# Latents' squares in buffers of their own, four of them summed by TensorE, small inputs and second modulations issued later, in a block of a diffusion backbone on one core

## The chip, the core and the metric

The kernel runs on one core of one Trainium2 chip. A core has five engines with a queue of instructions each, which run beside one another and meet at semaphores: TensorE (PE in the profile; its weight loads are listed apart as PEld) multiplies matrices and writes to PSUM, VectorE (DVE) and ScalarE (ACT) work on vectors, GpSimd (POOL) helps, and SyncE (SP) issues most of the DMAs. The metric is the device time of one execution in microseconds (us); lower is better. Everything is float32.

## The reference

The block has one layer. It takes 512 latent tokens x and 256 context tokens ctx of width 2048, and a condition c with its counterpart c_ctx. What is changed here is the beginning of the layer: RMSNorm of both streams, modulated by adaLN, and the first products of the combined input projection.

```python
mod = (c_act @ w_mod + b_mod)[:, None, :]
mod_c = (cc_act @ w_mod + b_mod)[None, None, :]
sh1, sc1, gt1, sh2, sc2, gt2 = jnp.split(mod, 6, axis=-1)
h = rmsnorm(x, g_norm1) * (1 + sc1) + sh1
hc = rmsnorm(ctx, g_norm1) * (1 + csc1) + csh1
lat_in, lat_gates = project_heads(h, w_in, gla_w_lr, gla_b_lr, mlstm_b_gate)
ctx_in, ctx_gates = project_heads(hc, w_in, gla_w_lr, gla_b_lr, mlstm_b_gate)
```

`rmsnorm` divides each token by the root of the mean of its 2048 squares. `project_heads` is one product with `w_in`, split among four heads of gated linear attention (GLA) and four of mLSTM. Scans over the tokens, an output projection, a SwiGLU MLP with a 3x3 convolution, and a last RMSNorm follow.

## The kernel before

Activations lie with their channels on the partitions: the latents are 16 tiles `xl[k]` of 128 channels x 512 tokens (256 KB each), the context is 8 tiles `xcp[j]` of two channel groups x 256 tokens. An operand of a product is split in two parts, a cast to the matrix format (`hi`) and the rest (`lo`), and each product is three matmuls: hi·hi, hi·lo, lo·hi (`mm3`). ACT makes the cast, DVE the rest, in `split` (L105 and L106).

All matmuls have one line, L111, and are told apart by tiles: `ss_l` and `ss_c` are the sums of squares of latents and context, `ps_m` the modulation products, `a` the projections. The projections' PSUM tiles come from two pools: six banks of `psA`, which hold the sums of head 0 for the whole first stage, and two banks of `psB`, taken in turn by everything else.

The order of the beginning is this.

- SP issues `cv` (the conditions), then two small inputs: the last columns of the constants (`cst`, L515, which hold the column of ones and the selectors) and `cols` (L516, norm weights and biases of the modulation). Then come the 16 latent tiles (L521), the 8 transfers of 512 KB of the first modulation weights (`mod_load`, L277), the first projection weights of head 1 and head 0 (`raw_h`, L195), the context (L419), the second modulation weights, and so on. The weights of each modulation are eight quarter tiles: four for the scale (region 1) and four for the shift (region 0); one such pair serves two channel groups.
- `stream_rstd` (L533) makes the reciprocal root: ACT squares a tile (L537), DVE adds it to a running total (L100), and at the end TensorE multiplies the total by a matrix of ones, which sums over the partitions and spreads the sum (`ss_l`). `mean_rsqrt` follows on ACT and DVE (L174 to L179). The squares take turns in two buffers, tag `sq`; the total has its own, tag `sqs`.
- `mod_rows` multiplies the modulation weights by the conditions (16 matmuls, each with 32 stationary columns and 256 moving ones, four side by side in the array; the page counts two instructions for each), ACT copies the result (L290), `mod_cols` turns it into columns by four small matmuls, and DVE finishes the scale `scol` (L302) or the shift `shcol` (L305).
- `modulate` applies the norm, the scale and the shift to two channel groups of one or both streams (L97, L557, L563) and splits the result into `hTh`, `hTl` (latents) and `hch`, `hcl` (context).
- `project_first` (L408) orders the products. Head 1's first products go through `psB` and are evicted to SBUF sums at once (`early_pair`, `early_group`); head 0's go to `psA` (`project_chunk`). Each has six groups: g = 0, 1 (q and k), 2, 3 (v) use the latents, g = 4, 5 the context. One round of 12 groups is one pair of channel groups (`kp`); there are 8 rounds, each with its own weights and its own pair of modulations.

Within `project_first` every matmul is pinned: TensorE runs them in the order in which the program names them. The other engines' queues are ordered by a planner, which simulates the program and takes an instruction when it is ready by its own estimate, the ones marked with high priority first; `tc.issue_after(ins)` keeps an instruction behind another on the same engine. Each queue then runs strictly in that order.

In the first round the program of before has: pair (g = 0, 1) and groups 2, 3 of head 1; group 0 of head 0; second scale product; group 1; its columns; the context's sum of squares; groups 2, 3; second shift product; group 4 of head 1; its columns; group 5 of head 1; group 4 of head 0; third scale product; group 5; its columns; then the second round.

Of the kernel before, what the change touches and what calls it, by code (L numbers as in the profile page):

```python
# [11 lines left out]
F32 = mybir.dt.float32  # L12
# [6 lines left out]
P = 128  # L19
HW = 256  # L20
D = 2048
KT = D // P
KP = KT // 2
T = 512
# [20 lines left out]
C_SA = C_SEG + T  # L45
# [38 lines left out]
def block_kernel(ctx: ExitStack, tc: tile.TileContext, a: dict, out: bass.AP):  # L84
# [323 lines left out]
    def project_first():  # L408

        banks = [acc(f"a0_{g}", BANKS[g]) for g in range(6)]  # L410
        both = accp.tile([P, CJ, T], F32, name="e0_c", tag="sums")
        early_both.append(both)
        sums = [None] * 4 + [both[:, j, 0 : DK + DV] for j in range(CJ)]
        stream_rstd(xl, rl, "l", T)
        for r in (1, 0):
            mod_cols(r, 0, *mod_rows(r, 0, mod_load(r, 0)))
        w1, w0 = (load_split(a["w_heads"][h, 0], f"h{h}_0") for h in (1, 0))
        for j in range(KT // 2):
            nc.sync.dma_start(xcp[j], a["ctxT"][j])  # L419
        raws = {r: mod_load(r, 1) for r in (1, 0)}  # L420
        with tc.high_priority():
            ins = modulate(0, "x")

        for _ in range(8):
            mm(banks[5][:, 0:P], ones, rl[:, 0:P], start=True, stop=True)
        early_pair(w1, sums)
        for g in range(2, 4):
            early_group(0, g, w1, sums)
        project_chunk(0, *w0, banks[0], 0)
        rows = mod_rows(1, 1, raws[1])  # L430
        project_chunk(0, *w0, banks[1], 1)
        mod_cols(1, 1, *rows)
        with tc.high_priority(), tc.issue_after(ins):
            stream_rstd([x.rearrange("p a b -> p (a b)") for x in xcp], rc, "c", TC)
            ins = modulate(0, "c")
        for g in range(2, 4):
            project_chunk(0, *w0, banks[g], g)
        rows = mod_rows(0, 1, raws[0])
        early_group(0, 4, w1, sums)
        mod_cols(0, 1, *rows)  # L440
        early_group(0, 5, w1, sums)
        with tc.issue_after(ins):
            modulate(1, "xc")
        w1 = load_split(a["w_heads"][1, 1], f"h1_1")
        for r in (1, 0):
            raws[r] = mod_load(r, 2)
        nc.sync.dma_start(cst[:, 0:C_SA], a["consts"][:, 0:C_SA])
        project_chunk(0, *w0, banks[4], 4)
        rows = mod_rows(1, 2, raws[1])
        project_chunk(0, *w0, banks[5], 5)  # L450
        mod_cols(1, 2, *rows)
        for kp in range(1, KP):
            for g in range(6):
                if g == 5 and kp + 1 < KP:
                    rows = mod_rows(0, kp + 1, raws[0])
                ins = early_group(kp, g, w1, sums)
                if g == 2:
                    with tc.issue_after(ins):
                        w0 = load_split(a["w_heads"][0, kp], f"h0_{kp}")
                    if kp + 2 < KP:  # L460
                        raws[1] = mod_load(1, kp + 2)
            if kp + 1 < KP:
                mod_cols(0, kp + 1, *rows)
                with tc.issue_after(ins):
                    modulate(kp + 1, "xc")
            for g in range(6):
                if g == 3 and kp + 2 < KP:
                    rows = mod_rows(1, kp + 2, raws[1])
                project_chunk(kp, *w0, banks[g], g)
                if g == 2 and kp + 1 < KP:  # L470
                    w1 = load_split(a["w_heads"][1, kp + 1], f"h1_{kp + 1}")
                    if kp + 2 < KP:
                        raws[0] = mod_load(0, kp + 2)
                if g == 3 and kp + 2 < KP:
                    mod_cols(1, kp + 2, *rows)
        return banks, sums
# [35 lines left out]
    rstd = xp.tile([P, T + TC], F32, name="rstd")  # L512

    nc.sync.dma_start(cv, a["cvec"])
    nc.sync.dma_start(cst[:, C_SA:], a["consts"][:, C_SA:])  # L515
    nc.sync.dma_start(cols, a["cols"])  # L516
    xl = [ytile(k, f"xl{k}") for k in range(KT)]
    xcp = [actp.tile([P, 2, TC], F32, name=f"xc{j}", tag=f"al{KT // 2 + j}") for j in range(KT // 2)]
    xc = [xcp[k // 2][:, k % 2, :] for k in range(KT)]
    for k in range(KT):  # L520
        nc.sync.dma_start(xl[k], a["xT"][k])  # L521
    S.preload_act_table_set("natural_log_exp_and_others")
    S.activation(ce, cv, AF.Exp, scale=-1.0)
    V.tensor_scalar(out=ce, in0=ce, scalar1=1.0, scalar2=None, op0=ALU.add)
# [6 lines left out]

    def stream_rstd(xs, o, name, n):

        tot = xp.tile([P, T], F32, name=f"sq_{name}", tag="sqs")
        for k, x in enumerate(xs):
            sq = tot if k == 0 else tmp.tile([P, T], F32, name=f"sq_{name}{k}", tag="sq")
            S.activation(sq, x, AF.Square)  # L537
            if k:
                add(tot, tot, sq)
        ps = psb(f"ss_{name}", (P, n))  # L540
        for i in range(0, T, n):
            mm(ps, ones, tot[:, i : i + n], start=(i == 0), stop=(i + n == T))
        var = tmp.tile([P, n], F32, name=f"var_{name}", tag="sq")
        scr = tmp.tile([P, n], F32, name=f"scr_{name}", tag="sq")
        mean_rsqrt(ps, D, var, scr, o)
# [968 lines left out]
```

## Time and profile before

| what | value |
|---|---|
| median of 3 runs | 2444.14 us (2443.68 to 2446.61) |
| the profiled execution's own time | 2443.46 us |
| its span, first to last instruction | 2441.7 us |
| PE busy in the span | 2401.8 us, 98% |
| DVE busy in the span | 1794.5 us, 73% |
| ACT busy in the span | 1003.2 us, 41% |

The profiled execution's own time is 1.76 us above its span (what lies around the first and the last instruction) and 0.68 us below the median of the runs. Times within the span count from its start. In a timeline a row has the start, the busy time, the engine, the line, the operation, the tile written and the tiles read, the count of instructions merged in the row, and in brackets how long the engine was idle before it and what ended that. PE's durations are modelled from the start of a matmul to the end of its pipeline, so a row of one PE instruction overlaps the next; the distance between starts is what it costs in a stream. The chain of waits is followed back from the end: each piece is what the next one waited for.

### The profile page before, as it was taken

The page shows a single profiled execution, that of the slowest core. Times are in us where ns is not written, and L with a number is a line of the kernel's source. Part 1 is how long each engine was busy: PE and PEld are TensorE (multiplying, and loading weights), DVE is VectorE, ACT ScalarE, POOL GpSimd, SP SyncE. Part 2 cuts the span into 40 slices and gives each one's busy share as a digit, 9 for nine tenths or more (in the row PEclk, how much of TensorE's full clock was granted, in tenths as well). Part 3 has the DMA queues.
Part 4 walks back from the last instruction along what each step waited for, and adds up shares of the span by engine and source line. Part 5 has one row for each costly group of instructions (what it writes and reads, how often), then busy time and mean ns, then how long its engine had stood idle before and what let it go on. Part 6 is the DMA issues. An engine that isn't in the chain of part 4 may idle for free.

```text
span 2441.7 us, 38643 instructions
## 1 busy us (share of the span) xinstructions
PE 2401.8 (98%) x15410; PEld 2166.8 (89%) x15410; DVE 1794.5 (73%) x2876; ACT 1003.2 (41%) x1494; POOL 176.3 (7%) x221
## 2 busy tenths in 40 slices
PE   6999999999999999999999999999999999999998
PEld 4888999899988888888898989898999999999997
DVE  6566856655456586769987878878787878787886
ACT  4225533222232232246544444444444444444445
POOL 0000000000000000000101010101011111111021
PEclk9999999999999999999999999999999999999999
DMA  9741111233455788833646464545555555545474
GB/s 384 288 173 56 46 53 44 78 121 113 138 185 191 239 316 279 287 129 111 146 131 154 116 148 124 145 127 138 139 130 142 135 139 126 144 125 151 113 190 130
DMA packets 122487, 373.67 MB, mean 153 GB/s; under 512 B 13912, under 2 KB 19010, under 8 KB 122306
## 3 DMA queue, kind: packets, MB, share of 16 engines
q1 hardware_dynamic: 95298, 318.75, 39.7%
q0 software_dynamic: 25920, 51.40, 11.7%
q8 instruction: 121, 1.98, 0.3%
q10 hardware_dynamic: 1088, 1.05, 0.1%
q14 instruction: 60, 0.49, 0.1%
HBM read 320.80 MB, written 50.34 MB: 152 GB/s over the span
## 4 chain that ended last, share of the span: by engine, by line
PE 84%; issue 6%; DVE 5%; DMA 2%; ACT 1%; POOL 0%; SPq 0%; DVEq 0%; POOLq 0%; ACTq 0%
PE a L111 18%; PE uv L111 16%; PE ug L111 15%; PE dn L111 14%; PE ga L111 7%; PE wo L111 7%; PE po L111 2%; PE ps_m L111 2%; DVE cv L1281 1%; DMA raw_uv<-in_w_up 1%; PE sl L111 1%; DVE lo_d L106 1%; PE st L111 1%; PE cst L111 1%; DVE ex L94 0%
## 5 line engine op out<-in xcount | busy, mean ns | idle before, releaser
L111 PE MATMUL dn<-gh,lo_d 128*128 128x512 f32 x672 | 263.0, 391 | 0.9 <-DVE lo_d L106 0.7
L111 PE MATMUL dn<-gh,hi_d 128*128 128x512 f32 x672 | 261.9, 390 | 0.0
L111 PE MATMUL dn<-gl,hi_d 128*128 128x512 f32 x672 | 261.7, 389 | 0.0
L1281 DVE SCALAR_TENSOR_TENSOR cv<-pads,cwt,cv 128x512 f32<-128x512 f32 x344 | 238.9, 745 | 0.6
L1335 POOL DMA_DIRECT2D x2d<-st x160 | 139.9, 929 | 1141.7 <-ACT st L1334 1061.0
L106 DVE TENSOR_TENSOR lo_buv<-sum_uv,hi_buv 128x1024 fp32r<-128x1024 f32 x80 | 97.9, 1224 | 99.8 <-ACT hi_buv L105 99.7
L322 DVE SCALAR_TENSOR_TENSOR raw_m<-raw_m,crow 128x1024 f32<-128x1024 f32 x128 | 154.6, 1229 | 1.2 <-DMA raw_m<-in_w_mod 1.2
L111 PEld LDWEIGHTS dn<-gh,lo_d 128*128 128x128 f32 x672 | 126.1, 188 | 30.8 <-DVE lo_d L106 4.8
L111 PE MATMUL a<-hi_h,hTh 128*128 128x256 f32 x512 | 151.6, 296 | 0.5 <-ACT e L404 0.5
L111 PEld LDWEIGHTS dn<-gl,hi_d 128*128 128x128 f32 x672 | 126.2, 188 | 26.0
L111 PEld LDWEIGHTS dn<-gh,hi_d 128*128 128x128 f32 x672 | 126.2, 188 | 25.4
L111 PE MATMUL a<-lo_h,hTh 128*128 128x256 f32 x512 | 144.8, 283 | 0.0
L111 PE MATMUL a<-hi_h,hTl 128*128 128x256 f32 x512 | 144.7, 283 | 0.0
L105 ACT CAST hi_d<-raw_d 128x1024 fp32r<-128x1024 f32 x86 | 88.6, 1031 | 132.0 <-PE ug L111 70.3
L106 DVE TENSOR_TENSOR lo_d<-raw_d,hi_d 128x1024 fp32r<-128x1024 f32 x86 | 102.8, 1195 | 48.2 <-ACT hi_d L105 47.5
L111 PE MATMUL ug<-bth,hi_bug 128*128 128x256 f32 x480 | 136.9, 285 | 0.0
L111 PE MATMUL uv<-bth,lo_buv 128*128 128x256 f32 x480 | 136.0, 283 | 0.8 <-DVE lo_buv L106 0.8
L111 PE MATMUL uv<-btl,hi_buv 128*128 128x256 f32 x480 | 135.9, 283 | 0.0
L111 PE MATMUL uv<-bqh,lo_auv 128*128 128x256 f32 x480 | 135.9, 283 | 0.0
L111 PE MATMUL ug<-bqh,hi_aug 128*128 128x256 f32 x480 | 135.9, 283 | 0.0
L111 PE MATMUL ug<-bqh,lo_aug 128*128 128x256 f32 x480 | 135.9, 283 | 0.0
L111 PE MATMUL uv<-bth,hi_buv 128*128 128x256 f32 x480 | 135.9, 283 | 0.0
(410 smaller groups left out, 7245.6 us busy)
## 6 DMA issues: line engine op xcount, KB each, us to landing
raw_m<-in_w_mod SPq DMA_DIRECT2D x192, 512.0 KB, 5.1
raw_d<-in_w_down SPq DMA_DIRECT2D x82, 512.0 KB, 3.5
raw_ug<-in_w_up SPq DMA_DIRECT2D x80, 512.0 KB, 3.5
x2d<-st POOLq DMA_DIRECT2D x160, 256.0 KB, 5.4
raw_uv<-in_w_up SPq DMA_DIRECT2D x80, 512.0 KB, 5.8
raw_h<-in_w_heads SPq DMA_DIRECT2D x64, 512.0 KB, 3.5
raw_ga<-in_w_gates SPq DMA_DIRECT2D x32, 512.0 KB, 3.6
raw_wo<-in_w_out SPq DMA_DIRECT2D x32, 512.0 KB, 4.8
```

What stands on the lines that cost most here:

```text
L105: cast[0] = S.copy(hi, x).ins
L106: return V.tensor_tensor(out=lo, in0=x, in1=hi.bitcast(F32), op=ALU.subtract).ins
L111: ins = PE.matmul(*args, **kw)
L322: V.scalar_tensor_tensor(out=x, in0=x, scalar=1.0, in1=crow[0], op0=ALU.mult, op1=ALU.mult, accum_out=mtot[:, at : at + 1])
L1281: V.scalar_tensor_tensor(out=t3, in0=src, scalar=w, in1=t3, op0=ALU.mult, op1=ALU.add)
L1335: nc.gpsimd.dma_start(x2d[k], t, accum_op=ALU.add)
```

## The change

- In `stream_rstd`, the latents' 16 squares get a buffer each. They are buffers of `actp` that later hold the split operands (`ah2` to `ah11` and `al2` to `al7`). The total is kept in the first of them. DVE adds the squares 1 to 11; the last four are not added. TensorE multiplies each of those by the ones itself and accumulates: squares 12, 13, 14, then the total, then square 15, five matmuls of 512 columns for one before. The context's eight squares are summed as before.
- The DMAs of `cst` (last columns) and `cols` are issued behind the 16 latent tiles, ahead of the modulation weights.
- In the first round TensorE's order becomes: pair and groups 2, 3 of head 1; groups 0, 1, 2 of head 0; the context's sum of squares; second scale product; group 3; its columns; group 4 of head 1; second shift product; group 5 of head 1; its columns; groups 4, 5 of head 0. The third scale product goes into the second round, behind its groups 0 and 1; its columns come behind group 2.

```diff
--- before.py
+++ after.py
@@ -426,34 +426,35 @@
         early_pair(w1, sums)
         for g in range(2, 4):
             early_group(0, g, w1, sums)
-        project_chunk(0, *w0, banks[0], 0)
-        rows = mod_rows(1, 1, raws[1])
-        project_chunk(0, *w0, banks[1], 1)
-        mod_cols(1, 1, *rows)
+        for g in range(3):
+            project_chunk(0, *w0, banks[g], g)
         with tc.high_priority(), tc.issue_after(ins):
             stream_rstd([x.rearrange("p a b -> p (a b)") for x in xcp], rc, "c", TC)
             ins = modulate(0, "c")
-        for g in range(2, 4):
-            project_chunk(0, *w0, banks[g], g)
+        rows = mod_rows(1, 1, raws[1])
+        project_chunk(0, *w0, banks[3], 3)
+        mod_cols(1, 1, *rows)
+        early_group(0, 4, w1, sums)
         rows = mod_rows(0, 1, raws[0])
-        early_group(0, 4, w1, sums)
+        early_group(0, 5, w1, sums)
         mod_cols(0, 1, *rows)
-        early_group(0, 5, w1, sums)
         with tc.issue_after(ins):
             modulate(1, "xc")
         w1 = load_split(a["w_heads"][1, 1], f"h1_1")
         for r in (1, 0):
             raws[r] = mod_load(r, 2)
         nc.sync.dma_start(cst[:, 0:C_SA], a["consts"][:, 0:C_SA])
-        project_chunk(0, *w0, banks[4], 4)
-        rows = mod_rows(1, 2, raws[1])
-        project_chunk(0, *w0, banks[5], 5)
-        mod_cols(1, 2, *rows)
+        for g in (4, 5):
+            project_chunk(0, *w0, banks[g], g)
         for kp in range(1, KP):
             for g in range(6):
                 if g == 5 and kp + 1 < KP:
                     rows = mod_rows(0, kp + 1, raws[0])
+                if kp == 1 and g == 2:
+                    rows = mod_rows(1, 2, raws[1])
                 ins = early_group(kp, g, w1, sums)
+                if kp == 1 and g == 2:
+                    mod_cols(1, 2, *rows)
                 if g == 2:
                     with tc.issue_after(ins):
                         w0 = load_split(a["w_heads"][0, kp], f"h0_{kp}")
@@ -512,13 +513,13 @@
     rstd = xp.tile([P, T + TC], F32, name="rstd")
 
     nc.sync.dma_start(cv, a["cvec"])
-    nc.sync.dma_start(cst[:, C_SA:], a["consts"][:, C_SA:])
-    nc.sync.dma_start(cols, a["cols"])
     xl = [ytile(k, f"xl{k}") for k in range(KT)]
     xcp = [actp.tile([P, 2, TC], F32, name=f"xc{j}", tag=f"al{KT // 2 + j}") for j in range(KT // 2)]
     xc = [xcp[k // 2][:, k % 2, :] for k in range(KT)]
     for k in range(KT):
         nc.sync.dma_start(xl[k], a["xT"][k])
+    nc.sync.dma_start(cst[:, C_SA:], a["consts"][:, C_SA:])
+    nc.sync.dma_start(cols, a["cols"])
     S.preload_act_table_set("natural_log_exp_and_others")
     S.activation(ce, cv, AF.Exp, scale=-1.0)
     V.tensor_scalar(out=ce, in0=ce, scalar1=1.0, scalar2=None, op0=ALU.add)
@@ -531,15 +532,26 @@
 
     def stream_rstd(xs, o, name, n):
 
-        tot = xp.tile([P, T], F32, name=f"sq_{name}", tag="sqs")
+        tot, tail = None, []
         for k, x in enumerate(xs):
-            sq = tot if k == 0 else tmp.tile([P, T], F32, name=f"sq_{name}{k}", tag="sq")
+            if len(xs) == KT:
+                tag = f"ah{2 + k}" if k < 10 else f"al{k - 8}"
+                sq = actp.tile([P, T], F32, name=f"sq_{name}{k}", tag=tag)
+            elif k == 0:
+                sq = xp.tile([P, T], F32, name=f"sq_{name}", tag="sqs")
+            else:
+                sq = tmp.tile([P, T], F32, name=f"sq_{name}{k}", tag="sq")
             S.activation(sq, x, AF.Square)
-            if k:
+            if k == 0:
+                tot = sq
+            elif k < 12:
                 add(tot, tot, sq)
+            else:
+                tail.append(sq)
         ps = psb(f"ss_{name}", (P, n))
-        for i in range(0, T, n):
-            mm(ps, ones, tot[:, i : i + n], start=(i == 0), stop=(i + n == T))
+        parts = [x[:, i : i + n] for x in tail[:-1] + [tot] + tail[-1:] for i in range(0, T, n)]
+        for i, part in enumerate(parts):
+            mm(ps, ones, part, start=(i == 0), stop=(i + 1 == len(parts)))
         var = tmp.tile([P, n], F32, name=f"var_{name}", tag="sq")
         scr = tmp.tile([P, n], F32, name=f"scr_{name}", tag="sq")
         mean_rsqrt(ps, D, var, scr, o)
```

## The prediction, made before the changed kernel was run

> **What bounds the kernel now.** I read the page first, then the waits of TensorE at the beginning, the timelines of DVE and ACT there, the landing of transfers, and last the chain of waits up to the second round.
>
> ```profile
> span 2441.7 us, 38643 instructions
> PE 2401.8 (98%) x15410; PEld 2166.8 (89%) x15410; DVE 1794.5 (73%) x2876; ACT 1003.2 (41%) x1494; POOL 176.3 (7%) x221
> ```
>
> TensorE is busy for 98% of the span, so it sets the time, and only what makes it wait counts. The change touches the first 60 us. These are TensorE's waits of the first 140 us (waiter, releaser: total, times, longest):
>
> ```profile
> PE ss_l L111 <- DVE sq_l L100: 19.4, 1, 19.4
> PE ps_m L111 <- ACT rows_m L290: 1.0, 2, 0.5
> PE a L111 <- ACT e L404: 0.5, 1, 0.5
> PE a L111 <- ACT e_c L390: 0.2, 1, 0.2
> ```
>
> Half of the 40 us without PE lie before the first matmul; after that under 2 us. So the question is by how much the stream of products starts earlier, and which waits come up behind it. First the squares, from ACT's and DVE's timelines:
>
> ```profile
> 3.50 0.56 DVE L589 CAST glr<-cst 2x768 fp32r<-2x768 f32 x1 [0.21 <-DMA cst<-in_consts]
> 9.26 2.02 ACT L537 ACTIVATE sq_l<-xl 128x512 f32<-128x512 f32 x3 [0.37 <-DMA xl<-in_xT]
> 17.81 0.63 ACT L537 ACTIVATE sq_l<-xl 128x512 f32<-128x512 f32 x1 [0.17 <-DVE sq_l L100]
> 9.92 9.45 DVE L100 TENSOR_TENSOR sq_l<-sq_l,sq_l 128x512 f32<-128x512 f32 x12 [0.30 <-ACT sq_l L537]
> 19.43 2.07 PE L111 MATMUL ss_l<-sq_l,cst 128*128 128x512 f32 x2 [19.43 <-DVE sq_l L100]
> 21.43 3.64 PE L111 MATMUL ps_m<-raw_m,cact 128*32 128x256 f32 x32
> 26.10 1.93 PE L111 MATMUL ps_m<-raw_m,cact 128*32 128x256 f32 x32
> 30.78 0.99 PE L111 MATMUL a<-hTh,hi_h 128*128 128x512 f32 x3
> 27.08 0.27 DVE L302 TENSOR_SCALAR scol<-ps_m,bp,cols 128x2 f32<-128x2 f32 x1
> ```
>
> DVE makes 12 adds in 9.45 us, 0.79 each. ACT, which first waits for the tiles, waits for DVE to free a buffer by its last square. The sum ends at 21.5; two modulation products follow, and the projections start at 30.78. The first modulation product took 3.64 us, the second, with the same 32 instructions, 1.93: TensorE is slow at first, by a factor of 1.89, and stays so from 19.43 to the last of 3.64 us of matmuls, some 5.4 us, at most 26.10-19.43=6.7. (The profile's granted clock is 1.00 there, so this slowness isn't in it.)
>
> Next the transfers: SP's issues, each followed by its KB and us to landing; then DMA share and GB/s in a table by stretch.
>
> ```profile
> 1.27 0.42 SPq L515 DMA_DIRECT2D cst<-in_consts  x1
> 2.21 9.21 SPq L521 DMA_DIRECT2D xl<-in_xT  x16
> 11.09 0.33 SPq L521 DMA_DIRECT2D xl<-in_xT  x1
> xl<-in_xT SPq DMA_DIRECT2D x1, 256.0 KB, 5.2
> 16.26 0.33 SPq L277 DMA_DIRECT2D raw_m<-in_w_mod  x1
> raw_m<-in_w_mod SPq DMA_DIRECT2D x1, 512.0 KB, 10.1
> cols<-in_cols SPq DMA_DIRECT2D x1, 74.0 KB, 2.0
> cst<-in_consts SPq DMA_DIRECT2D x1, 80.5 KB
> 20.00:30.00 10.00, 9.02 (x83) 4.33 (x82) 5.26 (x12) 3.01 (x5) 0.00 (x0) 1.00 1.03 416
> 30.00:60.00 30.00, 29.30 (x242) 23.67 (x241) 21.71 (x44) 15.86 (x30) 0.00 (x0) 1.00 1.03 415
> ```
>
> The last latent tile lands at 11.09+5.2=16.3, the last of the first eight modulation weights at 16.26+10.1=26.4, and the DMA engines are full throughout. That is the second limit: TensorE can't finish its second modulation product before 26.4 plus a last quarter (1.93/4=0.5).
>
> **The change part by part.**
>
> *Small inputs behind the latents.* The latents are issued 2.21-1.27=0.94 us earlier, so the last one lands at about 15.35. The two small inputs (154.5 KB) take about 0.4 us of the stream at 416 GB/s, so the ones land at 15.6 and the modulation weights at 26.4-0.94+0.4=25.85. Their readers: DVE's L530 and a cast at L589, which the planner may place among the adds (rival 1), and TensorE, whose sums can't start before the ones, at 15.6.
>
> *Squares in their own buffers.* ACT no longer waits for DVE: it follows the landings at 2.02/3=0.67 us a square and ends at 16.0 to 16.3. DVE has 11 adds: the fourth starts at 9.92-0.94=9.0, the eleventh ends at 9.0+8x0.79=15.3, 4.1 us earlier than 19.4. The buffers' later owners are operands of the second round, after 50 us.
>
> *Four squares on TensorE.* The same sum over 512 columns by ss_c, once TensorE is fast, costs 0.97 us (chain of waits, below); times 1.89 that is 1.83 cold, a little under the 2.07 of the lone one. Five run from 15.6. If TensorE stays cold for 5.4 us as before, until 21.0, then 5.4/1.83=2.95 are done, and 2.05x0.97=2.0 more end at 23.0. So the sum ends 1.5 us *later* than at 21.5, though the adds end earlier. The first modulation product is then fast, 1.93 for 3.64, which wins 1.7 back: the second starts 0.2 before 26.10, at 25.9, where its weights (25.85) just don't hold it. DVE's norm, from 21.5 to 27.35 before (its last interleaved row, 27.08+0.27), ends 1.5 later at 28.9, when the shift arrives. So the projections start 0.2 earlier, at 30.6. Ends: 1.1 earlier, if TensorE is fast so soon that the weights bind (their 25.85+0.5 and the product before it make the second end at 26.9, not 28.03); 0.1 later if it stays cold for 6.7 us.
>
> By the Trainium skill, page "TensorE: Matmul & The Clock Gate", Part 1, cold time is about 3.4 us of sustained activity, counted by a free-running window. The trace's 5.4 us is longer. By 3.4 the projections would start 1.1 us earlier instead of 0.2 (rival 2).
>
> *Second modulations moved.* TensorE's work is the same, so only new waits cost. The rows are pieces of the chain of waits (start, us) and DVE's timeline:
>
> ```profile
> 38.81 1.86 PE ps_m L111 x32
> 42.26 0.34 PE ps_m L111 x4
> 42.60 0.97 PE ss_c L111 x4
> 43.57 2.86 PE a L111 x24
> 46.44 1.86 PE ps_m L111 x32
> 49.58 0.50 ACT e_c L390
> 50.12 2.35 PE a L111 x12
> 52.48 1.86 PE ps_m L111 x32
> 54.34 1.24 PE a L111 x6
> 55.92 6.76 PE a L111 x42
> 47.06 0.73 ACT L105 CAST hch<-xc 128x256 fp32r<-128x256 f32 x2 [2.53 <-DVE xc L563]
> 47.50 0.76 DVE L106 TENSOR_TENSOR hcl<-xc,hch 128x256 fp32r<-128x256 f32 x2
> 50.05 0.34 DVE L305 TENSOR_SCALAR shcol<-ps_m,cols 128x2 f32<-128x2 f32 x2
> 52.93 1.23 DVE L106 TENSOR_TENSOR lo_h<-raw_h,hi_h 128x1024 fp32r<-128x1024 f32 x1 [0.37 <-ACT hi_h L105]
> 54.41 0.68 DVE L106 TENSOR_TENSOR hTl<-xl,hTh 128x512 fp32r<-128x512 f32 x1
> ```
>
> Their weights: all DMA slots are refilled as the stream needs them, since the issue runs 10 us ahead of the landing; products that come 2 to 4 us later use up a part of that lead, so I cost the queue on SP at nothing (if that lead were gone, each late transfer would cost its 1.26 us, 512 KB at 416 GB/s).
>
> The context first. Its chain runs from the end of ss_c, 43.57, to the first cast, 47.06+0.4, 3.9 us, and to the last rest, 48.26, 4.7 us. Before, two groups and a product cover it (2.86+1.86=4.7). After, there are a product, a group and the columns, 1.86+1.43+0.34=3.63, so group 4 of head 1 waits 0.25. In exchange the wait of 0.24 for the eviction e_c goes, since a modulation product now stands between groups 4 and 5.
>
> The latents' second pair of channel groups is the larger item. Before, shcol starts at 50.05 and the last hTl ends at 54.41+0.68=55.09, 5.04 us later, of which DVE works 4.67 and stands 0.37 for hi_h; the second round starts at 55.92, behind it. After, group 0 of head 0 ends at 38.8-0.2=38.6; +1.43+1.43+0.97 is 42.4, the end of ss_c. Group 4 starts at 42.4+3.9=46.3 and takes 1.17 (half of 2.35); +1.86 (shift product) +1.17 (group 5) +0.34 gives 50.8 for the columns. The cast hi_h needs the buffer that group 5 frees, which now comes earlier and fills the 0.37, so hTl ends at 50.8+4.67=55.5. Between the columns and the second round TensorE now has two groups, 2.4 us; before it had two more items, 1.86 and 0.34, and group 5. It reaches the round at 53.2 and would end its first group at 53.2+1.43=54.6 (a latents' group is half of 2.86); the last two of six matmuls wait for hTl and end at 55.5+0.48=56.0. That is a new wait of 1.35. Its ends: 0.6, where lo_h (1.23) is queued behind both hTl; 2.2, where the context's parts (four of 0.4) all come first and the 0.37 stays. Behind it come the moved third product and its columns, 2.2, so the point that was reached at 55.92+1.43=57.35 is reached at 58.2.
>
> *Sum.* -0.2 (start) +0.25 (context) -0.24 (e_c) -0.3 (gaps at switches between products, in the chain of before and not in my lengths) +1.35 (latents' operands) = +0.86, as 58.2-57.35. From there on TensorE streams as before. Against the profiled execution's 2443.46 this gives 2444.3; the median of the runs lies 0.68 above that execution, so 2445.0.
>
> **The rivals.** 0.2% is 4.9 us, and about what a measurement of this kernel can tell from no change.
>
> 1. *Small inputs block the adds (slower).* DVE takes its queue in order. If the planner puts L530 and L589 ahead of the adds, DVE stands until cols lands, about 15.8, then needs 0.7 for the two and 11x0.79=8.7: 25.2. Two sums follow, 1.9 fast or 3.7 cold: 27.1 to 28.9, so 5.6 to 7.4 later than 21.5, less 1.7 for a fast modulation product in the first case: +3.9 to +7.4. With the waits further on that is +5 to +8.5, 2449.1 to 2452.6. It decides only with more than five adds behind the two, since TensorE takes up the total at 15.6+3x1.83=21.1, and (21.1-16.5)/0.79=5.8. Against it: L589's row shows that the planner's landing of cst was right to 0.21 us, so it should see that squares are ready long before cols. The Trainium skill, same page and part, states that DVE and ACT are strict FIFO; the trace agrees, L589 held DVE for those 0.21 us.
> 2. *Fast early, operands early (a little faster).* The projections start 1.1 earlier instead of 0.2, and lo_h comes behind both hTl: 0.86-0.9-0.75=-0.8, 2443.3. No change by the bound.
> 3. *The squares bring nothing.* TensorE is cold for 6.7 us (+0.3) and DVE's scol of the second scale (two of 0.27) comes into the middle of the context's chain (+0.5): 0.86+0.8=1.7, 2445.8. Also no change.
> 4. *Another order far behind.* The planner sees a shifted beginning and orders ACT and DVE otherwise in the 2380 us that follow; nothing in the profile prices it, in either sign.
>
> **How the numbers follow.** Forecast 0.55, rival 2 0.15, rival 3 0.12: together 0.82, all within 0.2%. Rival 1: 0.09, slower. Rival 4 beyond the bound: 0.05 faster, 0.04 slower. Range: rival 2's 2443.3 less 2 for an order that differs behind, 2441.2; at the top it reaches rival 1's lower end, 2449.1. The forecast's own range, from the ends of its terms (-0.9 and -0.75, +0.3, +0.5 and +0.85), is 2443.3 to 2446.6.
>
> **What would show it.** Right: ACT's squares without DVE waits, ending near 16.3; ss_l as ten instructions from about 15.6 to 23; the first modulation product near 1.9 us; the projections at 30 to 30.7; a new wait of TensorE for hTl or lo_h at 53 to 55. Wrong: an idle DVE released by cst or cols among the adds; ss_l beyond 25; a DMA share below 1 before 60 us; a second round that starts with no wait.

## The result, and the profile after

The median after is 2448.05 us (20 runs, 2445.87 to 2451.57); before, on the same chips, 2443.40 (20 runs, 2440.58 to 2446.81). The ratio is 1.0016, 95% interval 1.0010 to 1.0022. By the ratio that is 3.9 us slower (2443.4 x 0.0016, from 2.4 to 5.4); the two medians themselves differ by 4.65. Both are inside the 0.2% (4.9 us) that counts as no change, and inside the predicted range, near its upper end. But the interval excludes no difference: the kernel after is slower, by less than the bound. The forecast difference was +0.86, so some 3 us came from something that the sum doesn't hold. First the page of the kernel after (span, then busy time by engine):

```profile
span 2446.6 us, 38631 instructions
PE 2407.6 (98%) x15418; PEld 2170.4 (89%) x15418; DVE 1793.0 (73%) x2872; ACT 1002.9 (41%) x1494; POOL 176.2 (7%) x221
```

These are TensorE's waits in its first 140 us (waiter, releaser: total, times, longest); the two rows that are as before, for `rows_m` and ACT's `e`, are left out:

```profile
PE ss_l L111 <- DMA cst<-in_consts: 15.4, 1, 15.4
PE a L111 <- DVE hTl L106: 1.0, 1, 1.0
...
PE a L111 <- DVE lo_h L106: 0.7, 1, 0.7
...
PE a L111 <- DVE e L392: 0.4, 1, 0.4
PE a L111 <- ACT hi_h L105: 0.2, 1, 0.2
PE a L111 <- DVE hcl L106: 0.2, 1, 0.2
```

TensorE's share is the 98% it was. The first wait is 4 us shorter (15.4 for 19.4) and that of 0.2 for `e_c` is gone, but five new ones stand behind. One of them, for `hTl`, is the one that the prediction priced. Now the beginning in the timelines of ACT, DVE and TensorE (start, length, engine, line, operation, tiles, count, idle time before):

```profile
6.54 9.17 ACT L544 ACTIVATE sq_l<-xl 128x512 f32<-128x512 f32 x14 [1.30 <-DMA xl<-in_xT]
7.21 7.86 DVE L100 TENSOR_TENSOR sq_l<-sq_l,sq_l 128x512 f32<-128x512 f32 x10 [1.24 <-ACT sq_l L544]
15.42 7.39 PE L111 MATMUL ss_l<-sq_l,cst 128*128 128x512 f32 x10 [15.42 <-DMA cst<-in_consts]
22.73 1.93 PE L111 MATMUL ps_m<-raw_m,cact 128*32 128x256 f32 x32
25.70 1.93 PE L111 MATMUL ps_m<-raw_m,cact 128*32 128x256 f32 x32
30.38 0.99 PE L111 MATMUL a<-hTh,hi_h 128*128 128x512 f32 x3
```

ACT runs through its squares without a wait for DVE and ends at 15.7, DVE's adds end at 15.07, the five sums run from 15.42 to 22.8, and the first modulation product is a fast one. The projections start at 30.38, 0.40 earlier than before. All of that is as forecast. The time is lost later, in the second round. These are some starts of TensorE's matmuls there, first of the kernel before:

```profile
55.78 0.48 PE L111 MATMUL a<-hTh,hi_h 128*128 128x512 f32 x1
58.37 0.39 PE L111 MATMUL a<-hTh,lo_h 128*128 128x512 f32 x1
60.02 0.28 PE L111 MATMUL a<-hi_h,hTh 128*128 128x256 f32 x1
65.98 0.48 PE L111 MATMUL a<-hTh,hi_h 128*128 128x512 f32 x1
66.52 0.39 PE L111 MATMUL a<-hTh,lo_h 128*128 128x512 f32 x1
```

and the same five matmuls of the kernel after, with the one that waits between the first and the second:

```profile
53.31 0.39 PE L111 MATMUL a<-hTh,hi_h 128*128 128x512 f32 x1
54.75 0.50 PE L111 MATMUL a<-hTl,hi_h 128*128 128x512 f32 x1 [1.05 <-DVE hTl L106]
57.40 0.39 PE L111 MATMUL a<-hTh,lo_h 128*128 128x512 f32 x1
62.06 0.39 PE L111 MATMUL a<-hi_h,hTh 128*128 128x256 f32 x1 [0.45 <-DVE e L392]
68.49 0.50 PE L111 MATMUL a<-hTh,hi_h 128*128 128x512 f32 x1 [0.23 <-ACT hi_h L105]
69.96 0.50 PE L111 MATMUL a<-hTh,lo_h 128*128 128x512 f32 x1 [0.73 <-DVE lo_h L106]
```

At the first two marks the kernel after still owes the third scale product and its columns, 1.86+0.36=2.22 us, which the kernel before has behind it; from the fourth row on they are done in both. So its position against before is 53.31+2.22-55.78=-0.25 at the start of the round, 57.40+2.22-58.37=+1.25 behind the wait for `hTl`, 62.06-60.02=+2.04 behind the wait for the eviction `e`, 68.49-65.98=+2.51 behind the wait for `hi_h`, and 69.96-66.52=+3.44 behind that for `lo_h`. (Each wait costs more than the idle time in brackets: in a stream, rows of 0.39 start 0.23 apart, so an overlap of 0.16 is lost as well, and the row behind the wait is one of 0.50.) So four waits in 17 us make nearly the whole loss. Why `lo_h` is late is seen in the queues of ACT and DVE. Before:

```profile
58.70 1.05 ACT L105 CAST hi_h<-raw_h 128x1024 fp32r<-128x1024 f32 x1 [3.92 <-DMA raw_h<-in_w_heads]
63.19 1.22 DVE L106 TENSOR_TENSOR lo_h<-raw_h,hi_h 128x1024 fp32r<-128x1024 f32 x1
65.82 0.56 DVE L392 SCALAR_TENSOR_TENSOR e_c<-a,e_c 128x384 f32<-128x384 f32 x1 [1.41 <-PE a L111]
```

After, with the copy of the modulation's rows ahead of the cast:

```profile
51.37 0.35 DVE L305 TENSOR_SCALAR shcol<-ps_m,cols 128x2 f32<-128x2 f32 x2 [2.36 <-PE ps_m L111]
67.12 0.37 ACT L290 COPY rows_m<-ps_m 128x256 f32<-128x256 f32 x1 [6.97 <-PE ps_m L111]
67.39 1.05 ACT L105 CAST hi_h<-raw_h 128x1024 fp32r<-128x1024 f32 x1
67.95 0.56 DVE L392 SCALAR_TENSOR_TENSOR e_c<-a,e_c 128x384 f32<-128x384 f32 x1 [2.55 <-PE a L111]
68.69 1.22 DVE L106 TENSOR_TENSOR lo_h<-raw_h,hi_h 128x1024 fp32r<-128x1024 f32 x1
```

Before, head 0's weights of the second round are cast when they land, at 58.70, and split at 63.19, between the two evictions. After, the planner has put the cast behind the copy of the third shift product's rows. ACT stands 6.97 us for that product with the cast queued behind it, and the rest `lo_h` stands on DVE behind the second eviction, for which DVE is idle for 2.55. No engine is short of time here: it is the order in two queues.

The position can also be read in one row: the start of the last of nine modulation products that lie between 70 and 160 us, the same one in every kernel. Before, then after (matmuls, their shortest/median/longest ns, first and last start):

```profile
L111 PE MATMUL ps_m<-raw_m,cact x288: 378/379/404, 70.3 to 154.0; 128*32 128x256 f32 x144
```

```profile
L111 PE MATMUL ps_m<-raw_m,cact x288: 379/379/403, 73.9 to 157.7; 128*32 128x256 f32 x144
```

After is 3.7 us behind at that mark, and its time 3.9 longer by the ratio (an interval of 2.4 to 5.4): what follows the mark adds nothing that the times could show.

### The profile page after: what moved, and what is told of

Its sections match the earlier page's. It is cut to its first block, busy times and chain, and to the rows that moved or that the text cites. A ratio compares the mean times of both kernels' runs of the same rounds, so it can differ in the third digit from the quotient of the medians.

```text
span 2446.6 us, 38631 instructions
## 1 busy us (share of the span) xinstructions
PE 2407.6 (98%) x15418; PEld 2170.4 (89%) x15418; DVE 1793.0 (73%) x2872; ACT 1002.9 (41%) x1494; POOL 176.2 (7%) x221
## 3 DMA queue, kind: packets, MB, share of 16 engines
q10 hardware_dynamic: 1088, 1.05, 0.1%
## 4 chain that ended last, share of the span: by engine, by line
PE 82%; issue 10%; DVE 4%; DMA 2%; ACT 1%; POOL 1%; SPq 0%; DVEq 0%; POOLq 0%; ACTq 0%
PE a L111 17%; PE dn L111 16%; PE uv L111 16%; PE ug L111 15%; PE ga L111 7%; PE wo L111 3%; PE po L111 2%; PE ps_m L111 1%; PE sl L111 1%; PE st L111 1%; PE cst L111 1%; DMA raw_m<-in_w_mod 1%; DVE cv L1293 0%; DVE ex L94 0%; DMA xl<-in_xT 0%
## 5 line engine op out<-in xcount | busy, mean ns | idle before, releaser
L111 PEld LDWEIGHTS dn<-gl,hi_d 128*128 128x128 f32 x672 | 126.2, 188 | 25.9
```

What stands on the lines that cost most here:

```text
L111: ins = PE.matmul(*args, **kw)
```

## The experiments

My theory was that the order of the second modulations costs some 4 us by three mechanisms (shift columns late for the second round; a PSUM bank; the order of cast, rest and evictions), and that the squares win a few tenths. The rivals were that the squares and small inputs cost something themselves, and that the planner orders the later stages otherwise (the prediction's rival 4). All runs together (start of the projections in the profile; position by the starts of equal matmuls against before at 75 us; span; median; ratio with interval, where there were several rounds):

| kernel | start | position | span | time | ratio |
|---|---|---|---|---|---|
| before | 30.78 | 0 | 2441.7 | 2443.40 | 1 |
| after | 30.38 | +3.6 | 2446.6 | 2448.05 | 1.0016 (1.0010 to 1.0022) |
| sq_only | 30.20 | -0.3 | 2440.2 | 2444.16 | 0.9997 (0.9988 to 1.0006) |
| order_only | 30.09 | +3.3 | 2445.4 | 2446.94 | 1.0008 (0.9999 to 1.0017) |
| third_back | 30.30 | +1.4 | 2442.1 | 2448.10 | 1.0011 (1.0002 to 1.0020) |
| cast_first | 30.10 | +3.8 | 2444.4 | 2450.10 | 1.0020 (1.0011 to 1.0029) |
| lo_first | 29.67 | +1.4 | 2445.8 | 2447.55, one run | |
| before_again | 30.31 | -0.1 | 2445.8 | 2447.51, one run | |
| sq_dve | 29.36 | -0.1 | 2443.6 | 2445.83, one run | |
| sq_warm | 29.63 | -0.7 | 2441.7 | 2443.38, one run | |
| mid_dve | 29.42 | -1.3 | 2441.9 | 2442.47 | 0.9996 (0.9987 to 1.0004) |
| mid_warm | 29.15 | -1.6 | 2442.1 | 2444.33 | 0.9997 (0.9988 to 1.0006) |

Each ratio is to the runs of the kernel before on the same chip, whose medians were 2443.40 (20 runs, beside the kernel after), 2444.03 (33 runs, the four from `sq_only` to `cast_first`), 2443.75 (one run, the four single ones) and 2444.74 (21 runs, the last two). The intervals are about 0.09% either way, 2.2 us (0.06% for the kernel after); single runs differ by more, for a reason that `before_again` shows. So mechanisms are judged by positions and waits, and the medians only by whether they agree.

**sq_only**: the squares and the small inputs as in the kernel after, `project_first` as before.

> The changed kernel with the old order of products in the first two rounds; the squares and the small inputs stay as changed. Theory (the loss comes from the moved modulation products): the projections start 0.4 us earlier than before, at 30.4, the second round starts at about 55.5, its head 0 part at 65.7 (before: 66.12), and from there TensorE stays 0.2 to 0.5 us ahead of the kernel before; time -0.4 us, no change. Rival (the squares and small inputs cost it, by a later sum or a disturbed DMA stream): head 0's part of the second round starts 3 to 4 us after 66.12, as in the changed kernel.

```profile
L111 PE MATMUL ps_m<-raw_m,cact x288: 379/379/403, 70.0 to 153.7; 128*32 128x256 f32 x144
```

The mark comes at 153.7, 0.3 earlier than before, and none of the new waits is there. The squares don't cost, and hardly win.

**order_only**: the reverse, the new order with the old squares and inputs. The edit of this and of `sq_only` is the two halves of the change:

```diff
@@ project_first: as after in order_only, as before in sq_only
-        project_chunk(0, *w0, banks[0], 0)
-        rows = mod_rows(1, 1, raws[1])
-        project_chunk(0, *w0, banks[1], 1)
-        mod_cols(1, 1, *rows)
+        for g in range(3):
+            project_chunk(0, *w0, banks[g], g)
...
@@ stream_rstd and the DMAs of cst and cols: as before in order_only, as after in sq_only
```

> The kernel before with the new order of products alone. Theory: the three new waits all appear (hTl 1.5 us, eviction 0.6, weights' cast 1.5), from 75 us on TensorE is 3.9 to 4.2 us behind the kernel before, time +4 us or a little more. Rival (squares and small inputs): within 0.5 us of the kernel before.

The waits and the mark of `order_only`:

```profile
PE a L111 <- DVE hTl L106: 1.1, 1, 1.1
PE a L111 <- DVE lo_h L106: 1.0, 1, 1.0
...
L111 PE MATMUL ps_m<-raw_m,cact x288: 379/379/403, 73.6 to 157.3; 128*32 128x256 f32 x144
```

The same waits but the small one for `hi_h`, and 3.3 us behind at the mark. The order alone makes the loss: counted from the start of the projections it is 3.3+0.7=4.0 here and 3.6+0.4=4.0 in the kernel after. (The time, with an interval from 0.9999 to 1.0017, would not show it.) At the mark it is smaller than I expected, since this execution started 0.7 earlier than that of before (30.09 against 30.78) with the same instructions up to there: the start varies by itself (`before_again` has 30.31), so the 0.40 that after starts earlier is no proof of a gain either.

**third_back**: from the kernel after, only the third scale product and its columns put back to where before has them.

```diff
-        for g in (4, 5):
-            project_chunk(0, *w0, banks[g], g)
+        project_chunk(0, *w0, banks[4], 4)
+        rows = mod_rows(1, 2, raws[1])
+        project_chunk(0, *w0, banks[5], 5)
+        mod_cols(1, 2, *rows)
```

> The changed kernel with the third scale product and its columns back between and behind groups 4 and 5 of head 0. Theory: the wait for hTl shrinks to 0, the wait for an eviction at 61 and the one for the weights' cast at 68 go (its cast stands ahead of the copy of the third shift product on ACT again), so from 75 us on TensorE is 0 to 0.5 us ahead of the kernel before; time -0.2 us. Rival (the second products' places alone cost it, by the context's chain): still 1 us or more behind.

Its ACT and TensorE around 56 us, and the mark:

```profile
55.92 0.40 ACT L105 CAST hch<-xc 128x256 fp32r<-128x256 f32 x1 [2.26 <-DVE xc L573]
56.23 0.37 ACT L290 COPY rows_m<-ps_m 128x256 f32<-128x256 f32 x1
56.65 0.61 PE L111 MATMUL ps_m<-cst,rows_m 128*128 128x2 f32 x4 [1.18 <-ACT rows_m L290]
...
L111 PE MATMUL ps_m<-raw_m,cact x288: 379/379/403, 71.7 to 155.4; 128*32 128x256 f32 x144
```

This removes the waits for `hTl`, for the eviction and for `lo_h` at a stroke, 2.2 us of the loss, but I had expected it to remove all of it. The copy of the product's rows now stands on ACT behind the last cast of the context, at the end of the same chain from the shift columns (here at 51.30), and TensorE waits 1.18 for the copy. So that chain takes its toll wherever TensorE first meets it. This part of the loss belongs to the second products, which lie later than before, not to the third one. That `third_back` is faster than the kernel after rests on the positions: its median is 4.1 us above that of before, and its interval, 1.0002 to 1.0020, holds a loss of 1.4 us as well as one of 3.9.

**cast_first**: from the kernel after, the copy of the third shift product's rows goes behind the cast `hi_h` of head 0 in ACT's queue.

```diff
-        with tc.high_priority():
+        with tc.high_priority(), behind(queue):
             S.copy(rows, ps)
...
-                    rows = mod_rows(0, kp + 1, raws[0])
+                    rows = mod_rows(0, kp + 1, raws[0], (cast[0],) if kp == 1 else ())
```

> The changed kernel with one order edge on ACT: the copy of the third shift product's rows queues behind the cast hi_h of head 0's second weights. Theory (that cast stood behind the copy though its weights had landed 9 us before): the wait of 1.5 us at 68 goes, the other two stay, and from 75 us on TensorE is 2.0 to 2.3 us behind the kernel before instead of 3.6. Rival (the cast waits for its weights or its buffer): no difference, 3.6.

```profile
59.81 1.05 ACT L105 CAST hi_h<-raw_h 128x1024 fp32r<-128x1024 f32 x1
67.70 0.56 DVE L392 SCALAR_TENSOR_TENSOR e_c<-a,e_c 128x384 f32<-128x384 f32 x1 [2.55 <-PE a L111]
68.91 1.22 DVE L106 TENSOR_TENSOR lo_h<-raw_h,hi_h 128x1024 fp32r<-128x1024 f32 x1
...
L111 PE MATMUL ps_m<-raw_m,cact x288: 379/379/403, 74.1 to 157.9; 128*32 128x256 f32 x144
```

A miss. The cast comes at 59.81, 7.6 us earlier, and TensorE isn't served any sooner: on DVE the rest is still queued behind the second eviction, which starts at 67.70 after 2.55 idle, and now also behind another instruction that the planner put ahead of it (`xl`, L97, 0.68 us from 68.18). The mark is 3.9 behind; counted from the start of the projections this is 0.5 worse than the kernel after. So the cast's place alone is not the cause.

**lo_first**: `cast_first`, and the second of the two evictions behind the rest `lo_h` in DVE's queue.

```diff
-                ins = early_group(kp, g, w1, sums)
+                ins = early_group(kp, g, w1, sums, (parted[0],) if (kp, g) == (1, 5) else ())
```

> The kernel of cast_first with one more order edge, on DVE: the eviction of group 5 of head 1 in the second round queues behind the rest lo_h of head 0's second weights. Theory (DVE stood idle before 67.7 with lo_h behind an eviction that waited for TensorE): lo_h runs near 63, TensorE's wait of 1.6 us for it at 70 goes, and from 75 us on TensorE is 1.5 us less behind than in cast_first: 2.3 us behind the kernel before (start counted alike) instead of 3.8. Rival (lo_h is late for another reason): no difference.

```profile
64.63 1.22 DVE L106 TENSOR_TENSOR lo_h<-raw_h,hi_h 128x1024 fp32r<-128x1024 f32 x1
...
L111 PE MATMUL ps_m<-raw_m,cact x288: 378/379/404, 71.8 to 155.4; 128*32 128x256 f32 x144
```

The rest is made at 64.63 in the 2.55 us in which DVE stood idle, the wait for `lo_h` is gone, and the mark comes 2.5 us earlier than in `cast_first`, of which the start accounts for 0.43. That is some 2 us against `cast_first`; against the kernel after the two edges together win 1.4 (1.4+1.1=2.5 us behind, counted from the start, for 4.0), the step from 2.04 to 3.44 above. It was paid for instructions in the wrong order in two queues with idle time, and the cast had to come early too: in the kernel after it ends only at 68.44.

**before_again**: the kernel before, unchanged, once more with a profile, to see what two executions of one program differ by.

> The kernel before, unchanged, to see how far the same program's beginning moves from one execution to another. If the start of the projections (30.78 in the first profile, 30.09 in the run with the new order alone, whose beginning is the same program) moves by 0.7 us by itself, the gain that the squares bring at the start can't be read to better than that. Expected: projections between 30.0 and 30.8, the same distances between TensorE's products behind them.

The mark, and then two stretches far behind in a table (bounds, length, busy time of PE, PEld, DVE, ACT and POOL with instructions, PEclk, the DMA share and GB/s):

```profile
L111 PE MATMUL ps_m<-raw_m,cact x288: 378/379/404, 70.2 to 154.0; 128*32 128x256 f32 x144
470.00:477.60 7.60, 6.99 (x59) 6.38 (x58) 6.67 (x22) 1.99 (x7) 0.00 (x0) 1.00 0.22 69
477.60:481.10 3.50, 3.50 (x11) 3.13 (x11) 1.69 (x8) 1.48 (x3) 0.00 (x0) 0.52 0.00 0
```

and the second of the two stretches in the first execution of before:

```profile
477.60:481.10 3.50, 3.50 (x18) 3.04 (x18) 2.35 (x8) 1.48 (x3) 0.00 (x0) 1.00 0.00 0
```

From the second round to 477 us the two agree within 0.1 us. There the granted clock falls to 0.52 for 3.5 us in one of them (11 matmuls for 18), which costs 1.6, and the same happens around 1075 us, for 2.3. At the end the spans differ by 4.1, with nothing changed. Every trace but the first of before has such a step at one or both of these places (after has one of 1.4 near 1075), so what a single span shows behind 450 us says nothing about a change of this size, and an order that differs far behind isn't needed to explain the times.

**sq_dve**: `sq_only`, with all sixteen squares added by DVE, one sum on TensorE.

```diff
-            elif k < 12:
+            elif k < 12 or len(xs) == KT:
```

> The kernel of sq_only with all sixteen squares of the latents added by DVE again, in their own buffers; one sum on TensorE. Theory (five sums on a cold TensorE take longer than DVE's four adds): DVE ends its adds at 18.2, the one sum runs from 18.3 to 20.4, 2.1 us earlier than the 22.6 of sq_only, the first modulation product is slow again (3.6), and the projections start 0.4 to 0.8 us earlier than in sq_only, at 29.4 to 29.8. Rival (it is the weights' landing alone that sets the start): no difference, 30.2.

Its second scale product, and the mark:

```profile
39.88 0.64 PE L111 MATMUL ps_m<-raw_m,cact 128*32 128x256 f32 x8 [0.59 <-DMA raw_m<-in_w_mod]
...
L111 PE MATMUL ps_m<-raw_m,cact x288: 379/379/403, 70.2 to 154.0; 128*32 128x256 f32 x144
```

The start is at 29.36 (29.42 in `mid_dve`, which begins alike), 0.8 earlier than in `sq_only` and 0.3 to 1.0 earlier than in the five executions with four squares on a cold TensorE. The adds ended at 18.6, 0.4 later than I expected, because the planner put the cast of a small input (L600, 0.56 us from 17.31) ahead of the last add: rival 1 of the prediction, in small. But nothing of the early start is left at the mark. The second scale product, in its old place, now waits for its weights, and its last quarter starts at 39.88, when the full stream of transfers has delivered it. This is the limit behind the limit: with the old order, most of an earlier start is handed to the next transfer.

**sq_warm**: `sq_only`, with eleven products of latent tiles ahead of the sums, whose results nothing reads.

```diff
+        for k in range(2, 13):
+            mm(banks[5][:, 0:256], xl[k][:, 0:P], xl[k][:, 0:256], start=True, stop=True)
```

> The kernel of sq_only with eleven small products of latent tiles, whose result nobody reads, ahead of the sums, so that TensorE is fast when the sums come. Theory: the five sums take 0.97 each, from 15.4 to 20.3, the first modulation product ends at about 22.2, and the second is bound by the landing of its last weights at 25.7: it ends at 26.2 and the projections start at 28.9, 1.3 earlier than in sq_only. The second scale product then waits for its weights at 39.6 (up to 1.2 us), so that at 75 us no more than 0.5 us of it are left. Rival (TensorE isn't slow for lack of use): sums of 1.8 as before, start 30.2.

```profile
16.03 4.53 PE L111 MATMUL ss_l<-sq_l,cst 128*128 128x512 f32 x10 [1.33 <-DMA cst<-in_consts]
26.25 0.64 PE L111 MATMUL ps_m<-raw_m,cact 128*32 128x256 f32 x8 [0.59 <-DMA raw_m<-in_w_mod]
```

The five sums take 4.53 us for 7.39, as the reading of a cold TensorE foretells. The gain is then cut at the next landing, as I had expected, but the last quarter could start only at 26.25, for weights expected at 25.7, and the start is 29.63 for 28.9. (That the second modulation product is held by its weights is the prediction's other end for the start.) At the mark 0.7 are kept, more than expected, since the second scale product waits less here: its last quarter starts at 39.36, for 39.88 in `sq_dve`.

**mid_dve** and **mid_warm**: these put the two findings together. The beginning is that of `sq_dve` or `sq_warm`; of the second modulations only the scale product moves, by one group, so that its weights have landed, and the shift product with its columns stays where before has it.

```diff
-        project_chunk(0, *w0, banks[0], 0)
-        rows = mod_rows(1, 1, raws[1])
-        project_chunk(0, *w0, banks[1], 1)
-        mod_cols(1, 1, *rows)
+        for g in range(2):
+            project_chunk(0, *w0, banks[g], g)
...
-        for g in range(2, 4):
-            project_chunk(0, *w0, banks[g], g)
+        rows = mod_rows(1, 1, raws[1])
+        project_chunk(0, *w0, banks[2], 2)
+        mod_cols(1, 1, *rows)
+        project_chunk(0, *w0, banks[3], 3)
```

> All sixteen squares added by DVE in buffers of their own, small inputs behind the latents, and of the second modulations only the scale product moved: from between the groups 0 and 1 of head 0 to between 1 and 2, its columns behind 2; everything else as in the kernel before. Theory (with the old order an early start is given back at the second scale product, because its last weights land at 39.2 to 39.9 whatever the start; the shift columns may not come later): projections start at 29.2 to 29.9, no wait of the second scale product for its weights, no wait of over 0.5 for hTl or lo_h, and the lead is kept: 0.8 to 1.4 us ahead of the kernel before at 75 us. Time 0.03 to 0.06% shorter, within the interval. Rival (the lead is lost anyway, at the shift columns and the operands of the second round): a new wait for hTl or lo_h of about 1, and within 0.3 us of the kernel before at 75 us.

> The same order (second scale product one group later than before) with the last four squares on TensorE and eleven unread products of latent tiles ahead of the sums. Theory: projections start at 29.5 to 29.9, no wait of the second scale product for its weights, 0.8 to 1.3 us ahead of the kernel before at 75 us; the time 0.03 to 0.06% shorter, within the interval. Rival: the lead of 0.65 that the old order kept with the same beginning stays as it is, because another wait comes up for hTl or lo_h.

The mark of `mid_dve`, then of `mid_warm` (some records are missing in both; the last start is the same product's):

```profile
L111 PE MATMUL ps_m<-raw_m,cact x276: 379/379/403, 69.6 to 152.7; 128*32 128x256 f32 x138
```

```profile
L111 PE MATMUL ps_m<-raw_m,cact x268: 379/379/403, 69.8 to 152.4; 128*32 128x256 f32 x134
```

No wait for `hTl`, `lo_h` or the weights of the second scale product is left, and the lead is kept: 1.3 and 1.6 us at the mark. So a move of the second modulations can help, by one group of one of them. As a time it is 0.05 to 0.07% and not to be told from none (0.9996, interval 0.9987 to 1.0004, and 0.9997, 0.9988 to 1.0006): faster than the kernel before is not shown. Against the kernel after, the intervals of the ratios don't overlap (up to 1.0006 here, from 1.0010 there), and the positions are 5 us apart.

## Why the prediction was right or wrong

The forecast, no measurable change at +0.86, holds by the bound and not by its sum: the loss is over four times the forecast one, and that it stays below 4.9 us is luck. The bound was also called about what a measurement can tell from no change; this one, of 20 runs, tells 3.9 us from none. Point by point:

- *Small inputs and squares*: right in each step. The ones landed for the sums at 15.42 (predicted 15.6), ACT ended at 15.7 (16.0 to 16.3), DVE's adds at 15.07 (15.3), and neither `cst` nor `cols` held up an add, so rival 1 didn't occur.
- *Four squares on TensorE*: right. The sums ended at 22.8 (23.0), later than before; the first modulation product took 1.93, and the second started at 25.70 (25.9). `sq_dve` and `sq_warm` confirm both halves: without the extra sums the start is at 29.36, with a warm TensorE the sums take 4.53. The start at 30.38 (30.6) is right in size, but the beginning of before starts them between 30.09 and 30.78 in three executions, and that of after between 29.67 and 30.38 in five, so the forecast gain of 0.2 couldn't have been told from nothing.
- *Weights of the second modulations*: costed at nothing, right for TensorE's waits in the kernel after. But one of the prediction's signs of being wrong did occur, a DMA share below 1 before 60 us (second but last figure of the row, after the clock and before the GB/s):

```profile
58.00:60.00 2.00, 2.00 (x35) 1.16 (x28) 0.52 (x1) 0.22 (x1) 0.00 (x0) 1.00 0.33 100
```

  Before, the share is 1.03 there. The third scale product frees the buffers of its weights 5.3 us later (it starts at 57.72 for 52.41), more than the 2 to 4 us that the prediction allowed for, and the stream of transfers runs short; `third_back`, with that product in its old place, has 1.03. No wait of TensorE for a transfer came of it in the first 140 us. And the row that would have told more wasn't looked for: the landing of the second scale weights is what caps a gain at the start in the old order.
- *The context and `e_c`*: right but for one wait. Group 4 of head 1 starts 0.63 behind the columns for 0.36, which is the forecast 0.25, and the wait for `e_c` is gone. A wait for `hcl` (0.2 idle, 0.4 by the starts) came on top; it is rival 3's. The second round was reached at 53.31 (53.2), from a start 0.2 earlier than forecast.
- *The latents' operands*: right in size, 1.35 for a wait of 1.05 that moved the stream by 1.5 (from -0.25 to +1.25), but in part because two errors offset each other. The shift columns were finished from 51.37 on, 0.6 later than predicted; from there DVE needed 4.26 us to the end of the last `hTl` for the forecast 4.67, since it left one of the context's parts (0.41) for behind, and `hTl` ended at 55.63 (55.5). And the wait fell on the second matmul of the group, for the first `hTl`, because DVE took `lo_h` ahead of both; the prediction had it on the last two of six.
- *"From there on TensorE streams as before"*: this is the step that failed. It holds 2.2 of the 3.4 us by which the stream is behind at 70 us: 0.8 up to the eviction (1.25 to 2.04; 0.6 of it is the wait itself, 0.95 from the columns to the next group for 0.36), and 1.4 at `hi_h` and `lo_h` (2.04 to 3.44). The first is the mechanism that the prediction itself used with the opposite sign in its paragraph on the context: where two groups of head 1 with only small columns between them take the two banks of `psB` in turn with the modulation product, the second waits for the eviction of the first. Moving the third product took its columns out from behind group 5 of head 0, which writes to `psA`, and put them between groups 2 and 3 of head 1. The second is an order that the planner chose for ACT and DVE. That is rival 4, which the prediction placed "far behind" and couldn't price; it happened 10 us behind the last line of the sum, where rows that were at hand (the rest at 63.19, which ends at 64.41, and its reader at 66.52) would have shown that there are 2.1 us to spare.

Rival 2 didn't come about: the sums took 7.39, so TensorE was cold for most of them, and `lo_h` came ahead of `hTl`. Of rival 3 one half did: DVE took `scol` of the second scale (46.01) ahead of the context's rests (46.39), which goes with the wait for `hcl`, 0.4 by the starts for 0.5 predicted; TensorE wasn't cold for longer. What stays open is how the planner came to its order: that it put the cast behind the copy is seen, its estimates aren't.

## What to carry to other kernels

When work on the bounding engine is moved by a few microseconds, follow each queue of the helping engines for as long as the shift lasts and not only to the first new wait: here more than half of the loss came from evictions, casts and rests behind the first new wait, some of them in queues that had idle time. Before paying for an earlier start, look for the next thing that doesn't depend on it (here a stream of transfers that was already full), and move only the consumer that meets it, by as little as will do. And compare positions of equal instructions right behind the change rather than whole spans, if one program's spans differ by more than the change is worth.

## What the runs showed of the hardware

The variation between executions of one program has a visible source. In `before_again` the granted clock is 0.52 from 477.6 to 481.1 and 1.00 on both sides, at a place where TensorE's stream has short gaps (in the stretch of 7.6 us ahead it is busy for 6.99); `mid_warm` and `sq_dve` lose 3.1 us at the same place, where the clock is at half for 6.8 us (in `sq_dve` from 476.7 to 483.5), and the first execution of before and `mid_dve` nothing. One such stretch costs 1.4 to 1.6 us and two in a row 2.3 to 3.1, so that two places, at 475 and 1075 us, with none, one or two of them could explain much of the 6 us between the fastest and the slowest run of one kernel; that the remaining runs differ by this was not looked at run by run. What in the stream sets a stretch off is not shown either: the same short gaps stand ahead of the place in the executions that lose nothing. The Trainium skill, page "TensorE: Matmul & The Clock Gate", Part 1, states a clock of half or full rate, set by the activity in windows of 3413 ns that run freely; the trace's 0.52 for 3.5 us agrees with both figures, and a free-running window would also be a reason why one program meets it in one execution and not in another. At the very beginning the same slowness by half (the first modulation product takes 3.64 us in one execution of before and 2.93 in the other) is not in the granted clock, which reads 1.00 there.
